# The output part of a linear-attention layer, traced in two pieces around the next step's matrix inverse

## The chip, the cores and the metric

The kernel runs on one core of one Trainium2 chip. Its time is the device time in microseconds of one execution; the time before is 3139.35 us, the median of three runs (3136.95 to 3140.87). Five engines work side by side, each through its own instruction stream in a fixed order: TensorE (PE; its weight loads are listed as PEld), VectorE (DVE), ScalarE (ACT), GpSimd (POOL) and SyncE (SP, which here only issues DMAs).

## The reference

Two layers over a sequence of 2048 tokens with 1024 channels. Only the first matters here. Its main branch is an RWKV-7 time mixing with 12 heads of width 64: each head keeps a 64 x 64 state, and per token

```
z = h @ a_w_in                      # projections, shifted in time by one token
state = state*w + sa (kk*a)^T + v k^T,   sa = state @ (-kk)
y = state @ r                       # per head
y = (y - mean(y)) * rsqrt(var(y) + LNX_EPS) * lnx_w + lnx_b
y = (y + bonus) * silu(gate)        # then one output projection with the memory branch
```

Beside it there is a cross-attention into 256 memory tokens; the second layer is a differential attention. Neither is touched.

## The kernel before

The first layer (`layer_a`) works on pairs of heads (6 pairs, index p) and on blocks of 512 tokens (4 blocks, in two halves of the sequence). One pair on one block is a `Step`; there are 24, in the order half, pair, block. A step treats its 512 tokens as 8 chunks of 64 and computes them in chunked form. Its parts are methods, and they are named here by what the prediction needs:

- `p1` (lines 334 to 395): the projections of the pair, each 24 matmuls of 128x512 (line 174), and elementwise work on them. `gate` is one more projection and a SiLU (lines 300 to 308). A step has four such projections, 96 matmuls, in all.
- `p2` (397 to 429): the chunk products `Gm` (PSUM tiles `pg`), transposes, and the bonus `bon`.
- `p3` (431 to 468): on DVE, the inverse of the 16 x 16 diagonal blocks. It ends in two DVE transposes, `T16` (line 462) and `TT16` (line 466).
- `p3b` (470 to 503): the rest of the inverse, a chain that goes back and forth between engines: PE products of `E1` and `T16` (line 481, first use) - ACT copy to `E1` (483) - PE products of `E1` and `TT16` (481, second use) - DVE add into `TT` (484) - DVE transpose `Ta` (487) - PE `invz` (494) - ACT copies (496) - PE `invr` (500) - DVE copies into `TT` (502).
- `p4` (508 to 564): PE transposes `atp` (520) and products `nvp` (528), ACT copies of both to `X` (522, 530), products with `TT` (`txp`, 539), and the chunk transition matrices (`mrp`, `ch`).
- `p4b` (566 to 590): the run over the 8 chunks, PE and ACT in turn (574, 575), then the output `ys` of the step (588, 590).
- `p5` (592 to 616): the normalisation of `ys` on DVE (597 to 608, with two small ACT operations at 605 and 606), then four PE transposes into `py` (611), an ACT scale and bias (613), the DVE addition of `bon` (614), the POOL product with the gate (615) and the store to DRAM, issued from POOL (616).

The main loop (lines 733 to 766) traces for step i: `p2` and `p3` of step i+1, `p4b` and `p5` of step i, `p3b` and `p4` of step i+1, and then `filler(i + 2)`, which holds the gate of step i+1 and `p1` of step i+2. The filler is where the long runs of projection matmuls come from.

Three things set the order. First, the place in the trace of the program is a rank: a list scheduler goes through a modelled run when the program is built and gives each engine the first-traced of the instructions that the model takes to be ready. So projection matmuls of the filler, traced last, stand between the products of `p3b` in PE's stream. On the chip that order is fixed, and an engine whose next instruction isn't ready waits. Second, the PSUM tiles of all these parts except the projections come from one ring of three buffers (tag "gm", `PS` at line 253). In the order of tracing, around the change, they are: `pvt`, `yp`, `yp`, `py`, two tiles `inv` (the two products of line 481), `invz`, `invr`, `atp`, `nvp`, `txp`, `txp`, `mrp`, `mrp`. The projections have their own three buffers (tag "pj"). Third, some tiles have one buffer only, `ys` among them, which the next step's line 590 writes again.

The steps 0, 10 and 11 differ from the others: the second half of the sequence starts with step 12, its input must first be normalised and transposed, and there are few projections left to put between.

Of the kernel before, what the change touches and what calls it, by code (L numbers as in the profile page):

```python
# [59 lines left out]
def hybrid_kernel(ctx, tc, S, HALF, x, mem, pv, cv, dist, postn, w_out, w_mkv, a_w, w2, a2, w_kv, b_w, out):  # L60
# [21 lines left out]
    def pc(name, i=0, n=1):  # L82
        return pvt[:, PV[name] + i:PV[name] + i + n]
# [41 lines left out]
    def split(ps, hi, lo):  # L125
        A.activation(hi, ps, AF.Copy)  # L126
        V.tensor_tensor(out=lo, in0=ps, in1=hi.bitcast(F32), op=ALU.subtract)
# [81 lines left out]
    def layer_a(ph):  # L209
# [31 lines left out]
        def T(shape, name, bufs=1, tag=None, dt=F32):  # L241
            return pa.tile(shape, dt, name=name, tag=tag or name, bufs=bufs)
# [10 lines left out]
        def PS(shape, name, tag="gm", bufs=3):  # L253
            if tag == "pj":
                return ppj.tile(shape, F32, name=name, tag="pj", bufs=3)
            return pps.tile(shape, F32, name=name, tag=tag, bufs=bufs)
# [69 lines left out]
        class Step:  # L326
# [263 lines left out]
                    A.activation(ys[:, :, hh], py[hh], AF.Copy)  # L590

            def p5(self):
                p, ys, sil = self.p, self.ys, self.sil
                bs = T([P, 8, 6], "bs", 1)
                y8 = ys.rearrange("p j h v -> p (j h) v")
                for i in range(8):
                    V.bn_stats(out=bs[:, i, :], in_=y8[:, i, :])
                sm = T([P, 4, 8], "sm", 1)
                V.tensor_tensor(out=sm[:, 0], in0=bs[:, :, 1], in1=bs[:, :, 4], op=ALU.add)
                V.tensor_tensor(out=sm[:, 1], in0=bs[:, :, 1], in1=bs[:, :, 4], op=ALU.subtract)  # L600
                V.tensor_tensor(out=sm[:, 2], in0=bs[:, :, 2], in1=bs[:, :, 5], op=ALU.add)
                V.scalar_tensor_tensor(out=sm[:, 3], in0=sm[:, 1], scalar=16.0, in1=sm[:, 1], op0=ALU.mult, op1=ALU.mult)
                V.tensor_tensor(out=sm[:, 2], in0=sm[:, 2], in1=sm[:, 3], op=ALU.add)
                V.tensor_scalar(out=sm[:, 0], in0=sm[:, 0], scalar1=0.5, scalar2=None, op0=ALU.mult)
                A.activation(sm[:, 3], sm[:, 2], AF.Ln, bias=eps_t[:, 1:2], scale=1.0 / 64)
                A.activation(sm[:, 3], sm[:, 3], AF.Exp, scale=-0.5)
                V.tensor_tensor(out=y8, in0=y8, in1=sm[:, 0, :, None].broadcast_to([P, 8, 64]), op=ALU.subtract)
                V.tensor_tensor(out=y8, in0=y8, in1=sm[:, 3, :, None].broadcast_to([P, 8, 64]), op=ALU.mult)
                py = PS([P, NJ, P], "py")
                for j in range(NJ):  # L610
                    nc.tensor.transpose(py[:, j, :], ys[:, j].rearrange("p h v -> p (h v)"), ident)
                yo = ys.rearrange("p j h v -> p (j h v)")
                A.activation(yo, py.rearrange("p j t -> p (j t)"), AF.Identity, bias=pc("lnx_b", p), scale=pc("lnx_w", p))
                V.tensor_tensor(out=yo, in0=yo, in1=self.bon, op=ALU.add)
                G_.tensor_tensor(out=yo, in0=yo, in1=sil, op=ALU.mult)
                G_.dma_start(out=y_dram[p * P:(p + 1) * P, self.t0:self.t0 + TB], in_=yo)

        def mem_w(m):
            return [load_a(c0) for c0 in (2432 + BR + m * P, 2432 + BR + MEMW + m * P)]

        def mem_q(m, half, bs, ws, between=lambda: None):
            for b in bs:
                def gate():
                    between()
                    return gate_silu(pj(ws[1], hTs[half, b]), W([P, TB], "g_sil"))
                store_q(0, m, half * NB + b, pj(ws[0], hTs[half, b]), gate, W)

        ths, steps = {}, []
# [28 lines left out]
        n = NHALF * NPAIR * NB  # L657
# [70 lines left out]
        def load_wo(hf):  # L728
            wo_w.append([ph.tile([P, KT, TB], F32R, name="wo" + t_, tag="h" + t_) for t_ in ("hi", "lo")])
            for c in range(0, 512, P):  # L730
                split_w(pa, w_out[0][:, hf * 512 + c:hf * 512 + c + P], None, *(t_[:, :, c:c + P] for t_ in wo_w[hf]), V, None, "iv", 4)

        for i in range(n):
            if i + 1 < n:
                steps[i + 1].p2()
                steps[i + 1].p3()
            steps[i].p4b()
            if i == n - 1:
                load_wo(0)

                yr0 = T([P, NC, P], "yr0", 2, "AR")[:, 0:NHB]
                nc.sync.dma_start(out=yr0, in_=y_dram[:, 0:P].rearrange("(k p) t -> p k t", p=P))
                y0 = T([P, KT, P], "yh0", 1, "BKT", F32R), T([P, KT, P], "yl0", 2, "AR", F32R)
                split(yr0, y0[0][:, 0:NHB], y0[1][:, 0:NHB])
                kv0 = T([P, 4, ML], "kb0", 2, "UV", F32R), T([P, 4, ML], "vm0", 2, "UV")[:, 0:2]
                G_.dma_start(out=kv0[0], in_=mem_d[0][0])
                nc.sync.dma_start(out=kv0[1], in_=mem_d[0][1])
                q0 = T([P, 2, 4, 2, P], "mq0", 2, "Gm", F32R)[:, 0]
                for dup in range(2):
                    G_.dma_start(out=q0[dup * 64:dup * 64 + 64], in_=q_d[0][0][0])  # L750
                g0 = T([P, 4, P], "mg0", 2, "bon")[:, 0:2]
                nc.sync.dma_start(out=g0, in_=q_d[0][1][0])
                for m in range(2):
                    mem_q(m, NHALF - 1, [NB - 1], ws[m])
                stl.close()
                op = OutProj(0, y_dram, x, x1_dram, 3, y0=y0, m0=(kv0, (q0, g0)))
            steps[i].p5()
            if i + 1 < n:
                steps[i + 1].p3b()
                steps[i + 1].p4()  # L760
            if i + 2 <= n:
                filler(i + 2)
            if i == n - 2:
                ws = [mem_w(m) for m in range(2)]
                for m in range(2):
                    mem_q(m, NHALF - 1, range(NB - 1), ws[m])
# [508 lines left out]

    ph = ExitStack()
    op = layer_a(ph.enter_context(pool_(name="ph", bufs=NB)))
    const2 = ctx.enter_context(pool_(name="const2", bufs=1, side="right"))
    ones = const2.tile([P, P], F32, name="ones")
# [103 lines left out]
```

## Time and profile before

| | before |
|---|---|
| median of 3 runs | 3139.35 us (3136.95 to 3140.87) |
| the profiled execution, its own time | 3131.17 us |
| its span | 3129.4 us |
| granted TensorE clock, mean | 0.979 |
| PE busy | 2944.0 us (94%) |
| DVE busy | 1794.5 us (57%) |
| ACT busy | 1504.3 us (48%) |
| POOL busy | 840.2 us (27%) |

The span runs from the first to the last recorded instruction; the 1.8 us around it belong to the execution's own time. The profiled execution was 8.2 us faster than the median of the three timed runs. A busy PE is one with a matmul under way by the profile, whose matmul ends are modelled; where successive matmuls overlap it counts as busy throughout, and the idle time in brackets ahead of an instruction is what is left. Steps 0 to 23 of the first layer end between 180 us and 1462 us of the span, about 50.2 us apart in the regular stretches.

### The profile page before, as it was taken

How to read it: one execution, taken by the hardware profiler on the slowest of the kernel's cores; microseconds unless marked ns; L12 is line 12 of the kernel's file. 1: busy time of each engine (PE TensorE's matmuls, PEld its weight loads, DVE VectorE, ACT ScalarE, POOL GpSimd, SP SyncE). 2: the span in 40 equal slices, each digit the busy share in tenths (PEclk: the TensorE clock that was granted, in tenths of full speed). 3: DMA queues.
4: the chain of work that ended last, by engine and by line, in shares of the span. 5: the costliest groups of instructions: out<-in, count | busy, mean ns of one | idle time of the engine just before them, and what ended most of it. 6: DMA issues, size and time to landing. Idle time of an engine off the chain costs nothing. (4 is left out here: it accounts for less than half of the span.)

```text
span 3129.4 us, 57336 instructions
## 1 busy us (share of the span) xinstructions
PE 2944.0 (94%) x22378; PEld 2390.8 (76%) x22378; DVE 1794.5 (57%) x4728; ACT 1504.3 (48%) x3310; POOL 840.2 (27%) x881
## 2 busy tenths in 40 slices
PE   6889999997899999998999999999999999998999
PEld 4767777776677777777777798888887888786777
DVE  6566767655676767673565311101118988887554
ACT  5545454545545454444454513213226777776443
POOL 3143423432243433431001212302212222323000
PEclk8899999998899999999999999999999999999999
DMA  3211000122011000115544533433355455543453
GB/s 119 78 33 37 28 24 23 39 61 84 26 30 37 28 24 24 38 45 142 147 135 127 147 86 91 118 86 92 102 164 123 101 113 115 122 85 103 129 153 116
DMA packets 262895, 264.13 MB, mean 84 GB/s; under 512 B 16736, under 2 KB 203232, under 8 KB 262496
## 3 DMA queue, kind: packets, MB, share of 16 engines
q1 hardware_dynamic: 234464, 193.87, 21.4%
q0 software_dynamic: 28160, 66.60, 10.4%
q8 instruction: 176, 2.88, 0.4%
q14 instruction: 95, 0.78, 0.1%
HBM read 179.14 MB, written 81.26 MB: 83 GB/s over the span
## 5 line engine op out<-in xcount | busy, mean ns | idle before, releaser
L174 PE MATMUL pj<-hhi,wh 128*128 128x512 f32 x928 | 389.6, 420 | 9.2 <-ACT sil L301 2.6
L174 PE MATMUL pj<-hhi,wl 128*128 128x512 f32 x928 | 375.3, 404 | 0.6 <-POOL wl L123 0.6
L174 PE MATMUL pj<-hlo,wh 128*128 128x512 f32 x928 | 368.5, 397 | 0.0
L123 POOL TENSOR_TENSOR wl<-wraw,wh 128x512 fp32r<-128x512 f32 x160 | 210.5, 1325 | 497.2 <-ACT wh L122 477.3
L1200 DVE CUSTOM_DVE_ANT_0 E<-s,dist 128x512 f32<-128x512 f32 (+1 forms) x480 | 276.1, 605 | 35.0 <-PE s L1198 28.9
L174 PE MATMUL pj<-bh,wh 128*128 128x512 f32 x672 | 262.8, 391 | 0.0
L174 PE MATMUL pj<-bh,wl 128*128 128x512 f32 x672 | 262.6, 391 | 0.0
L174 PE MATMUL pj<-bl,wh 128*128 128x512 f32 x672 | 262.5, 391 | 0.0
L1205 ACT ACTIVATE E<-E,nm 128x1920 f32<-128x1920 f32 (+7 forms) x192 | 229.4, 1199 | 59.1 <-DVE nm L1203 58.6
L174 PEld LDWEIGHTS pj<-hhi,wh 128*128 128x128 f32 x928 | 175.8, 189 | 63.7 <-ACT sil L301 8.9
L1238 PE MATMUL o<-th,vs 128*128 128x256 f32 (+1 forms) x864 | 211.0, 376 | 2.3 <-ACT th L1231 0.9
L1197 PE MATMUL s<-ks,qd 128*128 128x512 f32 (+1 forms) x480 | 205.6, 432 | 2.2 <-DVE mx L1200 1.2
L174 PEld LDWEIGHTS pj<-hhi,wl 128*128 128x128 f32 x928 | 175.4, 189 | 40.7 <-POOL wl L123 1.5
L174 PEld LDWEIGHTS pj<-hlo,wh 128*128 128x128 f32 x928 | 176.2, 190 | 38.8 <-issue 5.5
L122 ACT ACTIVATE wh<-wraw 128x512 fp32r<-128x512 f32 x160 | 100.3, 627 | 217.0 <-PE pj L174 139.4
L1238 PEld LDWEIGHTS o<-th,vs 128*128 128x128 f32 x864 | 153.9, 189 | 38.3 <-ACT th L1231 18.8
L1198 PE MATMUL s<-ks,qd 128*128 128x512 f32 (+1 forms) x480 | 176.1, 373 | 0.0
L174 PEld LDWEIGHTS pj<-bh,wh 128*128 128x128 f32 x672 | 126.7, 189 | 26.4 <-DVE ot L936 0.3
L174 PEld LDWEIGHTS pj<-bh,wl 128*128 128x128 f32 x672 | 126.6, 188 | 26.3
L174 PEld LDWEIGHTS pj<-bl,wh 128*128 128x128 f32 x672 | 126.6, 188 | 26.1
L1231 ACT ACTIVATE th<-tr 128x512 f32<-128x512 f32 (+1 forms) x216 | 113.2, 568 | 44.1 <-PE tr L1228 43.7
L1208 DVE SCALAR_TENSOR_TENSOR E<-E,nm,E 128x1920 f32<-128x1920 f32 (+7 forms) x96 | 132.1, 1376 | 0.9
(421 smaller groups left out, 6983.8 us busy)
## 6 DMA issues: line engine op xcount, KB each, us to landing
wraw<-in_a_w SPq DMA_DIRECT2D x118, 256.0 KB, 2.9
qd<-qd_d POOLq DMA_DIRECT2D x48, 512.0 KB, 7.0
mq<-mq POOLq DMA_DIRECT2D x64, 256.0 KB, 4.6
yr<-y_dram SPq DMA_DIRECT2D x32, 384.0 KB, 5.0
ks<-ks_d POOLq DMA_DIRECT2D x24, 512.0 KB, 7.0
xt<-in_x SPq DMA_DIRECT2D x16, 512.0 KB, 5.5
x_dram<-ot SPq DMA_DIRECT2D x16, 512.0 KB, 4.3
wraw<-in_b_w SPq DMA_DIRECT2D x32, 256.0 KB, 3.0
```

Of the source, the lines that this page charges most:

```text
L122: A.activation(hi[:, ks], raw, AF.Copy)
L123: eng.tensor_tensor(out=lo[:, ks], in0=raw, in1=hi[:, ks].bitcast(F32), op=ALU.subtract)
L174: mm(ps, lhsT=w[a_][:, k, wcol], rhs=h[b_][:, k, tsl], start=n == 0, stop=n == 3 * KT - 1)
L1197: mm(ps[:, f:f + w_], lhsT=qd[:, 0, c, qs], rhs=k_[:, c, 0:w_], start=True, stop=False)
L1198: mm(ps[:, f:f + w_], lhsT=qd[:, 1, c, qs], rhs=k_[:, c, 0:w_], start=False, stop=True)
L1200: V.tensor_tensor_reduce(out=e[:, kb * 512:kb * 512 + w], in0=ps[:, 0:w], in1=dt_[:, u0:u0 + w], scale=-SLOPES[h], scalar=3.0e38, op0=ALU. ...
L1205: A.activation(E[c][:, 0:nk], E[c][:, 0:nk], AF.Exp, bias=nm[:, c:c + 1], scale=-1.0, accum_out=nm[:, 2 + c:3 + c])
L1208: V.scalar_tensor_tensor(out=E[0][:, 0:nk], in0=E[1][:, 0:nk], scalar=nm[:, 5:6], in1=E[0][:, 0:nk], op0=ALU.mult, op1=ALU.add)
L1231: A.activation(th[:, 0:w], ps[:, 0:w], AF.Copy)
L1238: mm(po[:, oc], lhsT=vs[kt // 4][:, kt % 4, :], rhs=th[:, rc], start=n == 0, stop=n >= nmm - 2, skip_group_check=True)
```

## The change

`p5` ends after the normalisation. The rest, from the transposes to the store, becomes a method of its own, `p5b`, and the loop traces it after `p3b` of the next step and ahead of its `p4`. No instruction is added or taken away. In the ring of PSUM buffers `py` now comes after `invr` and before `atp`. For the last step nothing comes between the two parts.

```
             def p5(self):
-                p, ys, sil = self.p, self.ys, self.sil
+                ys = self.ys
...
                 V.tensor_tensor(out=y8, in0=y8, in1=sm[:, 3, :, None].broadcast_to([P, 8, 64]), op=ALU.mult)
+
+            def p5b(self):
+                p, ys, sil = self.p, self.ys, self.sil
                 py = PS([P, NJ, P], "py")
                 for j in range(NJ):
                     nc.tensor.transpose(py[:, j, :], ys[:, j].rearrange("p h v -> p (h v)"), ident)
...
             steps[i].p5()
             if i + 1 < n:
                 steps[i + 1].p3b()
+            steps[i].p5b()
+            if i + 1 < n:
                 steps[i + 1].p4()
             if i + 2 <= n:
                 filler(i + 2)
```

## Rows read from the trace of the kernel before

**Rows 1.** The page: engine busy time, share of the span, instructions.
```profile
PE 2944.0 (94%) x22378; PEld 2390.8 (76%) x22378; DVE 1794.5 (57%) x4728; ACT 1504.3 (48%) x3310; POOL 840.2 (27%) x881
```
**Rows 2.** Stages: start and end, length, each engine's busy time, granted clock, DMA.
```profile
282.00:735.00 453.00, 428.77 (x4528) 343.72 (x4528) 294.92 (x786) 220.41 (x490) 163.74 (x150) 1.00 0.14 41
735.00:882.00 147.00, 116.34 (x1135) 92.67 (x1135) 95.50 (x254) 71.42 (x166) 39.76 (x38) 0.87 0.13 40
```
**Rows 3.** Waits of PE, 180 to 1442 us: total us, times, longest.
```profile
PE py L611 <- DVE ys L608: 24.0, 23, 2.3
PE inv L481 <- DVE T L462: 13.9, 3, 6.1
...
PE invz L494 <- DVE Ta L487: 4.3, 10, 1.4
...
PE pj L174 <- ACT sil L301: 2.6, 10, 0.3
```
**Rows 4.** PE in step 4, in order: start, length, operation [idle before, releaser].
```profile
397.03 0.50 PE L174 MATMUL pj<-hhi,wh 128*128 128x512 f32 x1 [0.26 <-ACT sil L301]
...
398.98 0.40 PE L174 MATMUL pj<-hhi,wl 128*128 128x512 f32 x1
400.59 0.63 PE L611 MATMUL py<-cvt,ys 128*128 128x128 f32 x4 [1.22 <-DVE ys L608]
401.15 1.15 PE L481 MATMUL inv<-T,E 64*64 64x64 f32 x32
...
403.37 1.15 PE L481 MATMUL inv<-TT,E 64*64 64x64 f32 x32
...
409.06 1.09 PE L520 MATMUL atp<-cvt,AR 128*64 128x128 f32 x16
410.09 1.15 PE L528 MATMUL nvp<-UV,Gm 64*64 64x64 f32 x32
```
**Rows 5.** DVE in the same step.
```profile
395.62 0.17 DVE L603 TENSOR_TENSOR sm<-sm 128x8 f32<-128x8 f32 x1
...
395.82 1.08 DVE L462 STREAM_TRANSPOSE T<-X 128x512 f32<-128x512 f32 x1
...
398.60 1.07 DVE L466 STREAM_TRANSPOSE TT<-X 128x512 f32<-128x512 f32 x1
399.52 0.92 DVE L608 TENSOR_TENSOR ys<-ys,sm 128x512 f32<-128x512 f32 x1
...
409.90 0.84 DVE L502 COPY TT<-invr 32x256 f32<-32x256 f32 x2
```
**Rows 6.** ACT in the same step.
```profile
395.67 0.63 ACT L122 ACTIVATE wh<-wraw 128x512 fp32r<-128x512 f32 x1 [2.70 <-PE pj L174]
396.21 0.29 ACT L605 ACTIVATE sm<-sm,eps_t 128x8 f32<-128x8 f32 x1
396.40 0.57 ACT L301 ACTIVATE sil<-pj 128x512 f32<-128x512 f32 x1
...
402.54 0.58 ACT L483 ACTIVATE E<-inv 128x512 f32<-128x512 f32 x1
```
**Rows 7.** DVE in step 5.
```profile
445.91 1.08 DVE L462 STREAM_TRANSPOSE T<-X 128x512 f32<-128x512 f32 x1
...
447.44 1.08 DVE L466 STREAM_TRANSPOSE TT<-X 128x512 f32<-128x512 f32 x1
```
**Rows 8.** PE in step 5.
```profile
451.00 0.63 PE L611 MATMUL py<-cvt,ys 128*128 128x128 f32 x4 [0.86 <-DVE ys L608]
```
**Rows 9.** PE in step 11.
```profile
831.83 0.66 PE L611 MATMUL py<-cvt,ys 128*128 128x128 f32 x4 [1.51 <-DVE ys L608]
...
842.03 1.97 PE L481 MATMUL inv<-T,E 64*64 64x64 f32 x32 [3.77 <-DVE T L462]
```
**Rows 10.** Two stretches after such waits, columns as in rows 2.
```profile
196.50:199.90 3.40, 3.40 (x36) 2.51 (x35) 0.82 (x3) 3.12 (x6) 1.27 (x1) 0.50 0.00 0
841.60:848.50 6.90, 6.47 (x70) 5.32 (x71) 3.63 (x8) 4.53 (x8) 1.36 (x3) 0.51 0.01 2
```

More of the change, by code (lines that the diff above doesn't have):

```diff
@@ L592, in p5 @@
             def p5(self):
-                p, ys, sil = self.p, self.ys, self.sil
+                ys = self.ys
                 bs = T([P, 8, 6], "bs", 1)
@@ L608, in p5, with p5b @@
                 V.tensor_tensor(out=y8, in0=y8, in1=sm[:, 3, :, None].broadcast_to([P, 8, 64]), op=ALU.mult)
+            def p5b(self):
+                p, ys, sil = self.p, self.ys, self.sil
                 py = PS([P, NJ, P], "py")
@@ L759, in layer_a @@
                 steps[i + 1].p3b()
+            steps[i].p5b()
+            if i + 1 < n:
                 steps[i + 1].p4()
```

## The prediction

> **What bounds the kernel now.** The page comes first: PE is busy 94% of the span, the next engine 57% [rows 1]. So time is won where PE idles, or where it works slowly. The stages tell how much idle time there is: from 282 to 735 us, nine regular steps, PE is busy 428.8 of 453.0 us at a full clock, which leaves 24.2 us, 2.7 us a step; from 735 to 882 us, around the turn to the second half of the sequence, it idles 147.0 - 116.3 = 30.7 us and the mean granted clock is 0.87 [rows 2]. Then the waits of PE say what ends the idle time. The largest group is exactly what is edited: the transposes into `py` wait for the last normalisation on DVE (line 608), 24.0 us in 23 waits. The second is the first product of `p3b` waiting for `T16`, 13.9 us, but in three waits only [rows 3]: the steps 0, 11 and 10.
>
> The regular steps come in two kinds, by the block. In even ones, step 4 for all nine, PE issues the last of nine projection matmuls at 398.98 and then stands 1.22 us for line 608; the product of `T16` follows behind the transposes at 401.15, the second product at 403.37 [rows 4]. In odd ones, step 5 for eight, the wait is 0.86 us (0.79 to 0.88) [rows 8]. The steps 9 and 21 wait 0.3 us, step 22 2.27.
>
> One more thing is to be seen in step 4. `T16` is complete at 395.82 + 1.08 = 396.90 [rows 5], 4.25 us before its product starts, and nine projection matmuls of lower rank stand between. The scheduler would have put the product ahead of them if it could. What held it is the ring of three PSUM buffers: its `inv` tile comes behind `py` there, so it has no buffer before `py` has one. That is what the change takes away.
>
> **The change, part by part.** No work is added: the four transposes (0.63 us of PE), the ACT operation, the addition, the product and the store are the same. PE has as many turns from projections to small matmuls as before, since the transposes go from the front of the first product to the front of `atp`. So PE's work is the same and the sum goes over its waits.
>
> *Removed.* Line 608's wait ahead of the transposes: 1.22 us in nine steps, 0.86 in eight. Behind the inverse the normalisation is long done. With it should go the 0.26 us that the projection at 397.03 waits for ACT [rows 4], since the product of `T16` will stand about there; and the 0.33 us by which `invz` waits for `Ta` in the nine even steps (3.0 of the 4.3 us in [rows 3]; 1.36 is step 10), because the scan that DVE does between `TT` and `Ta` there isn't ready yet when `TT` comes some 4 us earlier.
>
> *Added: a wait for `T16`.* DVE doesn't get faster, and where PE's order follows the modelled run it will now stand at the product. How long depends on how far the model is from the chip at that point, and ACT's order shows it. In step 4 ACT took the weight copy (line 122) at 395.67 first, then line 605 and then the gate's copy (301) [rows 6]. Line 122 waits for the end of the gate's projection. Line 605 needs line 603, and has the higher rank, so in the model 603 ended after 122 was taken and before it was through, that is 0 to 0.5 us behind the projection's end. On the chip 603 ended at 395.79 [rows 5], 0.1 us behind. The chip is on the model's time there, or ahead of it. `T16` takes 1.08 us from there. If the model gives it 0.6 (my estimate, from what the whole way to line 608 must take in the model: the nine matmuls and those of `lr` run from 395.7 to 399.2, so at most some 3 us, where the chip needs 4.65), the model has `T16` 0.7 to 1.2 us behind the projection and the chip 1.2. Bounds for the wait at the first product: 0, and 1.2 if it is put right behind the gate's projection. I take 0.25 in even steps and 0.3 in odd ones, nearest to what line 603 shows.
>
> *Added: a wait for `TT16`.* The second product needs `TT16`, 398.60 + 1.07 = 399.67 in step 4 [rows 5]. The first product would run from 397.0 to 398.15, ACT copies in 0.58 us [rows 6], and the model, which has `TT16` earlier, puts some three matmuls between: PE stands at the second product from about 398.9. That is a wait of 0.8; bounds 0 and 1.5 (399.67 less the first product's end). I take 0.9 with the latency. In odd steps `TT16` comes 1.53 us after `T16` [rows 7] instead of 2.77, and the ACT copy ends no earlier: 0.1.
>
> *Behind it.* The second product comes at about 399.8 instead of 403.4, and the whole chain with it, 3.6 us earlier. This gives nothing by itself: PE has projections to do in place of it, before or after. The transposes now stand between `invr` and `atp`, and delay `atp` by 0.6; the projections cover that too. On ACT line 613 (0.76 us) comes ahead of the copies to `X`, while PE does `atp` (1.09 us), which covers it. On POOL the product with the gate and the store come about as late as the second product now does plus 3 us; behind them there stand only weight splits of the filler, for which PE waits nowhere in [rows 3]. The buffer `ys` is written again 45 us later.
>
> *The ring.* `nvp` gets the buffer of `invr`, which DVE frees (line 502), where before it had that of `invz`. In step 4 line 502 ends at 410.74 [rows 5]; `nvp` would be issued 0.57 us later than the 410.09 of before [rows 4], at 410.66. So 0.1 us a step; bounds 0, and 1.2 if DVE has the scan (1.23 us in this step) under way. I take 0.1.
>
> *Sum of the regular steps.* Even: 1.22 + 0.26 + 0.33 go, 0.25 + 0.9 + 0.1 come: 0.56 us, nine times, 5.0. Odd: 0.86 goes, 0.3 + 0.1 + 0.1 come: 0.36, eight times, 2.9. Step 22: 2.27 goes, perhaps half comes back: 1.1. Steps 9 and 21: nothing. Together 9.0 us.
>
> *The three steps of the turn.* In step 11 PE waits 1.51 us for line 608 and then, with 25 matmuls between, 3.77 for `T16` [rows 9]. Taking the first wait away lets PE reach the second earlier and stand there longer, so nothing is won; the transposes (0.66 us) pass from a time when PE has to wait anyway to behind the inverse. In step 10 nothing is left to fill and they lengthen the chain, by 0.66 to 1.1 us. Step 0 is like step 11. I take 1 us of loss for step 10. The clock: after the waits in step 0 and step 11 it is at half, the 1.2 GHz level, for 3.4 and 6.9 us, with PE busy 3.40 and 6.47 us of these [rows 10]. One such stretch more, of 3.4 us, costs 1.7 us of work; I take 1 us for the two steps together, from 0 to 3.4.
>
> The Trainium skill (TensorE: Matmul & The Clock Gate, section "What's actually happening") says that the throttled state is the default and that activity releases it. By that rule the longer hole at `T16` (3.77 + 1.51 + 0.6 = 5.9 us in step 11) must lengthen the slow stretch in both steps, the full 3.4 us; by the rows alone the stretch stays as it is. The sum would be 4.6 us gained by the one, 8.0 by the other.
>
> In all 9.0 - 1 - 1 = 7.0 us are gained: 3124.2 us for the profiled execution of 3131.17 us (3122.4 of span). The median of the runs lies 8.2 us higher, and I carry the difference over to it: 3132.4, say **3132 us**.
>
> **The rivals.**
> *A: the forecast*, gains of 2 to 14 us. Chance 0.45.
> *B: the wait only moves.* PE's order is laid down by a model that is 1.5 us ahead of DVE by line 608, and what is saved there is stood out at `T16` and `TT16` in full. For it: in step 11 just that must happen; against it: line 603 is on time, and between it and line 608 other work can be put. 3139, within 4 us. Chance 0.19.
> *C: the waits vanish.* 24.0 less the 3.4 of the three steps of the turn and 0.6 of the steps 9 and 21, with 2.6 and 3.0: 25.6 us less 2: about 3115. It needs the first product to fall on or after `T16` on the chip. For it: 603 is early, if anything; against it: `TT16` falls 2.77 us later in even steps. Chance 0.15.
> *D: the ring and the order cost more than the wait.* With `nvp` bound to line 502, and line 502 behind the scan or a mix on DVE, PE stands up to 1.2 us in each of 20 steps; the model, in which the copies are short, doesn't fill the time. At 1.0 us each and with B's zero gain: 20 us, less what the odd steps escape, about 14 with the slow clock: 3153. It decides from the point where that wait is over 0.5 us, the mean gain of a step (9.0 / 20). For it: 502 comes within 0.1 us of `nvp` already. Against: DVE is idle between the parts of the inverse. Chance 0.18.
> *E: nothing changes in PE's order*, because something other than the ring holds the first product behind the transposes: 3139. Chance 0.03.
>
> **How the numbers follow.** About 0.2%, 6.3 us, is what a measurement of this kernel tells from no change. Faster by more: C and two thirds of A, 0.45. Within: the rest of A, B and E, 0.37. Slower: D, 0.18. The range goes from 3115, C's value, to 3147, short of D's: it leaves out half of C and rather more than half of D, 0.2. A alone would be 3125 to 3137.
>
> **What will show it.** In the profile after: the wait of line 611 for line 608 gone from the list; the first product of line 481 ahead of the transposes, some 4 us earlier after the end of `yp`; waits for `T16` and `TT16` on line 481 of together about 1.1 us in even steps and 0.4 in odd ones; the transposes between lines 500 and 520; PE idle from 282 to 735 us down by 4 us. I am wrong if line 481 still stands behind line 611, if its new waits reach 1.5 us a step, if line 528 waits for line 502 by more than 0.5, or if the stretch of the turn grows by more than 4 us.

## The result, and the profile after

The changed kernel takes **3159.3 us** (median of four runs, 3157.3 to 3160.32) against 3138.94 us for the kernel before in the same job: a ratio of **1.0064**, 95% interval 1.0051 to 1.0076. It is slower by about 20 us, where 3132 was forecast, 7 us faster; the time lies above the range.

From the page of the kernel after, the counterpart of [rows 1]:

```profile
PE 2967.7 (94%) x22378; PEld 2403.1 (76%) x22378; DVE 1786.8 (57%) x4728; ACT 1505.7 (48%) x3310; POOL 830.7 (26%) x881
```

The same instructions, and PE is *busy* 23.7 us longer. The spans of the profiled executions are 29.1 us apart (3158.5 and 3129.4), more than the medians, since the one before lay 8.2 us below its median. The stages, with the columns of [rows 2], in stretches that do about the same work as those of before (steps 1 to 9, the turn, steps 13 to 22):

```profile
290.00:757.00 467.00, 435.26 (x4499) 346.09 (x4496) 294.51 (x783) 218.50 (x486) 159.79 (x148) 0.97 0.14 40
757.00:904.00 147.00, 120.18 (x1157) 95.99 (x1155) 96.20 (x257) 72.30 (x168) 42.78 (x41) 0.86 0.14 41
904.00:1415.00 511.00, 479.04 (x5363) 379.23 (x5361) 345.28 (x930) 241.03 (x524) 183.80 (x174) 0.98 0.10 29
```

Before, the regular steps ran at a granted clock of 1.00 (share of the full 2.4 GHz, rounded); the last of these three stages was, in the kernel before:

```profile
882.00:1385.00 503.00, 471.65 (x5361) 376.75 (x5360) 348.77 (x931) 239.34 (x525) 188.57 (x175) 1.00 0.10 30
```

The count of matmuls and the idle time are nearly the same (5361 and 5363; 31.4 and 32.0 us), but it takes 8 us more, with the clock at 0.98. The waits of PE after, 180 to 1442 us (the counterpart of [rows 3]; line 611 is now line 614):

```profile
PE inv L481 <- DVE T L462: 27.7, 23, 6.1
PE ch L574 <- ACT S L575: 24.4, 33, 2.7
PE pg L406 <- DVE Gm L408: 11.1, 12, 1.7
...
PE inv L481 <- DVE TT L466: 3.9, 6, 1.5
...
PE pss L367 <- ACT rn L359: 2.5, 8, 0.6
...
PE invz L494 <- DVE Ta L487: 1.7, 2, 1.4
...
PE txp L539 <- ACT X L530: 0.5, 1, 0.5
```

The 24.0 us of the transposes into `py` have gone. In their place stand the wait for `T16` (13.9 before) and one that was small: the state products of `p4b` (line 574) waiting for the state that ACT copies (line 575), 24.4 us now and 5.2 before. The wait at `txp`, 9.7 us before, is all but gone. The two rows of the kernel before:

```profile
PE ch L574 <- ACT S L575: 5.2, 14, 2.4
...
PE txp L539 <- ACT X L530: 9.7, 20, 0.5
```

Where it happens is seen in PE's instructions. First the end of `yp` in the kernel before (step 4, just ahead of [rows 4]), then, in the kernel after, a step whose inverse goes as forecast (step 5):

```profile
391.90 0.33 PE L588 MATMUL yp<-S,RT 64*64 64x64 f32 x4
```

```profile
452.32 0.33 PE L588 MATMUL yp<-S,RT 64*64 64x64 f32 x4
457.22 1.15 PE L481 MATMUL inv<-T,E 64*64 64x64 f32 x32 [0.26 <-DVE T L462]
...
464.70 0.66 PE L614 MATMUL py<-cvt,ys 128*128 128x128 f32 x4
```

The first product of the inverse starts 4.57 us behind the end of `yp`; in the kernel before it was 8.9 us (392.23 to 401.15 in [rows 4]). The whole chain, with `p4` at its end, is some 4 us earlier. The next rows show what then follows `p4`, first in the kernel before (step 4, behind [rows 4]), then in the kernel after (step 3):

```profile
408.08 0.39 PE L174 MATMUL pj<-hhi,wl 128*128 128x512 f32 x1
408.40 0.73 PE L500 MATMUL invr<-TT,Ta 32*32 32x32 f32 x32
...
415.27 1.15 PE L563 MATMUL ch<-UV,BKT 128*64 128x64 f32 x32
416.35 1.12 PE L367 MATMUL pss<-rn,cvt 128*128 128x512 f32 x2
```

```profile
367.57 1.15 PE L563 MATMUL ch<-UV,BKT 128*64 128x64 f32 x32
...
370.15 0.39 PE L174 MATMUL pj<-hhi,wl 128*128 128x512 f32 x1
370.38 0.33 PE L574 MATMUL ch<-sb,MT 128*128 128x64 f32 x2
372.33 0.43 PE L574 MATMUL ch<-S,MT 128*128 128x64 f32 x2 [1.63 <-ACT S L575]
373.17 0.43 PE L574 MATMUL ch<-S,MT 128*128 128x64 f32 x2 [0.41 <-ACT S L575]
374.21 2.07 PE L367 MATMUL pss<-rn,cvt 128*128 128x512 f32 x2 [0.60 <-ACT rn L359]
...
376.51 0.63 PE L174 MATMUL pj<-hlo,wh 128*128 128x512 f32 x1
376.94 0.63 PE L174 MATMUL pj<-hhi,wl 128*128 128x512 f32 x1
```

The projection that ends at 408.5 in the one and at 370.5 in the other is `kx`, the first of the next `p1` in the trace. `pss` (line 367) is a matmul on an elementwise result of `kx`, and in the order of PE the projections `rx` and `vx` come behind it. In the kernel before, `pss` follows 7.9 us behind the end of `kx` (8.3 in the other kind of step): in that gap PE does the end of the inverse and all of `p4`, and waits less than 1 us in all. In the kernel after this differs from step to step. In every second one, as here, `p4` is over *before* `kx` ends. The gap from `kx` to `pss` is 3.7 us in the first half of the sequence and 2.9 in the second, and what the scheduler found for it are three state products of the next `p4b`. Two of them wait for ACT, here 1.63 and 0.41 us, and `pss` waits 0.60 behind them. In the steps between, `kx` still ends ahead of the last part of `p4`, and `pss` follows that without a wait, 4.9 us behind `kx` (step 4):

```profile
421.12 0.40 PE L174 MATMUL pj<-hhi,wl 128*128 128x512 f32 x1
...
425.36 1.15 PE L563 MATMUL ch<-UV,BKT 128*64 128x64 f32 x32
426.44 1.13 PE L367 MATMUL pss<-rn,cvt 128*128 128x512 f32 x2
```

There it is DVE that is late, with `T16`, ahead of the inverse of the same step:

```profile
408.61 1.97 PE L481 MATMUL inv<-T,E 64*64 64x64 f32 x32 [2.19 <-DVE T L462]
...
411.10 0.63 PE L174 MATMUL pj<-hhi,wh 128*128 128x512 f32 x1
```

Beside both waits the granted clock falls to half, 1.2 GHz instead of 2.4: the product of 1.15 us takes 1.97, `pss` takes 2.07 for 1.12, and projection matmuls start 0.43 us apart (376.51, 376.94) where 0.23 is usual. The windows say the same (columns as in [rows 2]):

```profile
374.40:377.80 3.40, 3.40 (x7) 2.04 (x8) 0.69 (x1) 0.72 (x2) 0.58 (x1) 0.53 0.32 95
408.60:412.00 3.40, 3.39 (x36) 3.05 (x37) 2.13 (x6) 1.95 (x4) 0.78 (x3) 0.54 0.31 89
```

Summed from the traces for each stretch from one end of `yp` to another (before, after; us):

| ends of `yp`, steps | matmuls | length | PE idle | PE busy | at half clock |
|---|---|---|---|---|---|
| 1 to 9 | 4288 | 405.0, 422.2 | 25.5, 32.0 | 379.5, 390.3 | 6.8, 34.1 |
| 9 to 12 (turn) | 1912 | 247.4, 249.8 | 32.4, 31.4 | 215.0, 218.4 | 37.5, 44.4 |
| 12 to 22 | 5360 | 503.2, 511.0 | 31.3, 32.0 | 471.8, 479.0 | 3.4, 17.1 |

The two regular rows are 25.1 us longer: 7.1 us more of idle time, and 18.0 us more of busy time for the same matmuls. The time at half clock is 41.0 us longer; half of that, 20.5, is about what the busy time gained. By the wait that stands next to each fall of the clock, 30.7 of the 51.2 us at half clock go with the state products, 10.2 with `T16`, and 10.2 with `pg`.

Of the 29.1 us there remain 4.4 us ahead of the end of `yp` in step 0, 2.6 won in step 1, 2.4 lost in the turn, and 0.1 won behind step 22. The 4.4 us are not the change's: up to 186 us of the span the instructions of PE, ACT, DVE and POOL stand in the same order in both kernels.

### The profile page after: what moved, and what is told of

It reads as the page before. It is cut to its first block, busy times and chain, and to the rows that moved or that the text cites. A ratio compares the mean times of both kernels' runs of the same rounds, so it can differ in the third digit from the quotient of the medians.

```text
span 3158.5 us, 57321 instructions
## 1 busy us (share of the span) xinstructions
PE 2967.7 (94%) x22378; PEld 2403.1 (76%) x22378; DVE 1786.8 (57%) x4728; ACT 1505.7 (48%) x3310; POOL 830.7 (26%) x881
## 4 chain that ended last, share of the span: by engine, by line
PE 71%; DVE 13%; ACT 7%; issue 4%; DMA 3%; POOL 1%; SPq 0%; ACTq 0%; DVEq 0%; POOLq 0%
PE pj L174 29%; PE po L930 10%; PE o L1243 5%; PE vps L1106 4%; PE s L1202 3%; PE s L1203 2%; PE tr L1233 2%; PE inv L481 2%; PE mo L866 1%; DMA wraw<-in_a_w 1%; DVE Ti L455 1%; DVE E L1205 1%; DVE itmp L453 1%; PE mpt L859 1%; PE pss L367 1%
## 5 line engine op out<-in xcount | busy, mean ns | idle before, releaser
L174 PE MATMUL pj<-hhi,wh 128*128 128x512 f32 x928 | 396.6, 427 | 8.5 <-DVE hlo L149 1.8
L1243 PEld LDWEIGHTS o<-th,vs 128*128 128x128 f32 x864 | 154.0, 189 | 37.9 <-ACT th L1236 18.6
```

Source lines behind the costliest of these rows:

```text
L174: mm(ps, lhsT=w[a_][:, k, wcol], rhs=h[b_][:, k, tsl], start=n == 0, stop=n == 3 * KT - 1)
L1243: mm(po[:, oc], lhsT=vs[kt // 4][:, kt % 4, :], rhs=th[:, rc], start=n == 0, stop=n >= nmm - 2, skip_group_check=True)
```

## The experiments

Theory T, formed from this: the change does shorten the chain, and the chain was what covered the elementwise work that follows `kx`. With less cover, PE meets a hole, and what fills or fails to fill it sets the time. At first T reached from `kx` to `pss` only; the way on from `pss` to the chunk products `pg` was added after a_rx_first and a_pss_gm had missed. The rivals: R1, the drawn-forward state products are themselves the cost; R2, the transposes and the buffer of `py` in the middle of the chain are.

### The state products held back (a_chunks_late)

The state products (line 574) may be issued on PE only behind the last transposes of `p2`, so none can be drawn ahead of `pss` (dots stand for code in between):

```
-                    nc.tensor.transpose(pv_[:, j, :], self.vx[:, j * P:(j + 1) * P], ident)
+                    Step.last = nc.tensor.transpose(pv_[:, j, :], self.vx[:, j * P:(j + 1) * P], ident)
...
-                    mm(ch[:, c, :], lhsT=MT[:, c, :], rhs=st[c], start=False, stop=True, skip_group_check=True)
+                    with tc.issue_after(Step.last.ins):
+                        mm(ch[:, c, :], lhsT=MT[:, c, :], rhs=st[c], start=False, stop=True, skip_group_check=True)
```

> The changed kernel, with the state products of the next step (line 574) held behind the last transposes of p2 on PE, in issue order only, so that none of them can be drawn forward. In the changed kernel every second step has three of them drawn forward into the time between the first projection and the product pss (line 367). Theory T (the inverse and p4 now end 3.6 us earlier, and so no longer cover the time that pss waits for the elementwise work on the first projection; the next projections have to wait for pss, which stands ahead of them in their PSUM ring): the idle time stays and turns up as a wait of line 367 in all regular steps, some 2.5 to 3.5 us in each of 20; 3155 to 3185 us. Rival R1 (the early state products themselves are the cost, by their waits and by what they do to the order of the next step): 3120 to 3137 us. Rival R2 (the new place of py in the ring of three buffers, and of the transposes between invr and atp, is the cost): 3153 to 3165 us, with no large wait of line 367.

3185.86 us (3183.93 to 3210.86), ratio 1.0181 (1.0136 to 1.0226), 0.9 us above T's range and far above those of R1 and R2: with nothing drawn forward the time rises, and a large wait stands at line 367. R1 is out, and R2 doesn't explain this wait. The waits of PE:

```profile
PE pss L367 <- ACT rn L359: 61.7, 20, 3.2
```

With the state products gone, `pss` waits 2.9 to 3.2 us in *each* of 20 steps, and stands 2.9 to 3.2 us behind `kx`, just as long as the elementwise work takes. Here the hole is in every step; in the changed kernel the state products stood in it in every second one and `p4` in the others.

This run also tells about the wait for `T16`: between the ends of `yp` 1 to 9 and 12 to 22 it comes to 17.2 us in the changed kernel, and here to 4.9 in as many waits (18, about 0.27 each). So the late `T16` comes with the drawn-forward order and isn't what makes the hole. How much of the 20 us it carries no run shows.

### The hole filled with matmuls that are thrown away (a_busy)

Twelve projection-sized matmuls write into the tile of `pss` just before it; their result is overwritten.

```
                 pss = PS([P, TB], "pss", "pj")
+                for k in range(0 if first else 12):
+                    mm(pss, lhsT=ws[0][0][:, k % KT, :], rhs=h[0][:, k % KT, :], start=True, stop=True)
```

> The changed kernel with 12 extra projection matmuls (2.7 us, of operands that are there, into the PSUM tile of pss, which pss then overwrites: work that is not used) ahead of pss in each step but those of the first pair. With them nothing is drawn forward, and PE's order is that of a_chunks_late but for the 12 matmuls, which stand where that kernel waits 3.1 us at pss. So PE waits as long, but working. Theory K (half of the loss is TensorE's clock, which falls to half after waits of 2 us and more, as it was for 51 us of the regular steps in a_chunks_late and 14 us in the kernel before): 3186 less 15 to 20, 3160 to 3173 us, granted clock of the regular steps near that of before. Rival (the wait alone counts, the slow clock falls into it): 3182 to 3192 us.

3164.04 us, ratio 1.0099 (1.0079 to 1.0119), as theory K expected. The state products stay behind `pss` here too, so a_chunks_late is the one to compare with: 22 us *less* with twelve matmuls *more* in each of 20 steps (240; the four steps of the first pair have none). First a_chunks_late, then a_busy, 300 to 740 and 900 to 1400 us:

```profile
300.00:740.00 440.00, 402.07 (x4280) 318.46 (x4280) 274.67 (x705) 202.07 (x437) 151.69 (x139) 0.98 0.12 35
900.00:1400.00 500.00, 455.83 (x4960) 359.56 (x4959) 330.28 (x884) 222.54 (x484) 169.75 (x162) 0.96 0.09 26
```

```profile
300.00:740.00 440.00, 426.18 (x4437) 339.65 (x4436) 275.46 (x713) 208.48 (x452) 152.99 (x143) 1.00 0.13 37
900.00:1400.00 500.00, 482.43 (x5355) 383.41 (x5351) 334.55 (x912) 234.99 (x511) 167.80 (x162) 1.00 0.09 27
```

The clock is whole again and the idle time more than halved (37.9 + 44.2 us to 13.8 + 17.6). A pair of steps took 105.8 us and takes 103.5: in the first half, 6.1 us of idle time and 1.7 of clock (half of 3.4) less, 5.4 of matmuls more (24 at 0.227, as they follow each other in this trace). The matmuls take up about the time that was idle; what is won is mostly the clock. By the Trainium skill (TensorE: Matmul & The Clock Gate, section "What's actually happening") throttling is the default and activity lifts it; the two kernels agree (a granted clock of 0.98 and 0.96, then 1.00).

The expectation's "after waits of 2 us and more" does not hold as a bound. In the kernel before, the clock fell to half beside single waits of 1.12 to 1.14 us at `pg` three times in the regular steps (at 278, 381 and 1282 us); in a_chunks_late it stayed full beside eight of the 3.23 us waits at `pss`.

### `rx` ahead of `pss` (a_rx_first, b_rx_first)

Useful work in the hole: the second projection traced ahead of `pss`, in the changed kernel and in the one before.

```
-                first = p == 0
+                first = True
```

> The changed kernel, with the second projection (rx) of every step traced ahead of pss, as the kernel has it already for the first pair: 24 projection matmuls (5.4 us) that need no pss. Theory T: the uncovered time is filled, no state product is drawn forward, PE loses its waits at lines 611, 574 and 367: 36 us less than with the waits, 3100 to 3127 us. R1: also 3105 to 3130, since nothing is drawn forward. R2: no lower than 3143 us, since the transposes and their ring are where they were.

3174.45 us, ratio 1.0122 (1.0107 to 1.0137).

> The control: the kernel before, with the same second projection ahead of pss. Theory T: there pss was covered by p4 already, so only the 0.5 us goes that PE waits at txp in each of 20 steps: 3122 to 3138 us. R1 and R2 the same. If it gains as much as the changed kernel does with it, the projection's place is worth that by itself and says nothing of the change.

3199.38 us, ratio 1.02 (1.018 to 1.0219). Both missed, 47 and 61 us above their ranges; the first lies where R2 had it. The rows of waits, of a_rx_first and of b_rx_first:

```profile
PE pg L406 <- DVE BK L383: 57.1, 21, 3.4
```

```profile
PE pg L406 <- DVE BK L383: 56.0, 21, 2.9
PE py L611 <- DVE ys L608: 20.1, 21, 1.5
```

`pss` doesn't wait any more, but the elementwise work goes on behind it (`rn`, `BK`, up to line 383), and only `vx` is left to do meanwhile. The hole has moved from `pss` to `pg`. The split's own part is visible beside it: 25 us between the two kernels.

### `pss` off the ring of the projections (a_pss_gm)

The tile of `pss` takes a buffer of the small tiles, so that `rx` can be ahead of it by one buffer more.

```
-                pss = PS([P, TB], "pss", "pj")
+                pss = PS([P, TB], "pss")
```

> The changed kernel, with pss in the ring of the small tiles (gm) instead of the projections' ring; the order of tracing is left as it is. Theory T: what held the projections back was that pss comes ahead of them in their ring, so freeing the ring is enough: 3100 to 3130 us, PE without waits at lines 574 and 367. R1: the same if nothing is drawn forward. R2: 3145 us or more. If projections are held by something else than the ring, 3153 to 3165 us.

3150.92 us, ratio 1.0043 (1.0028 to 1.0058): missed, though 8 us below the median of the change alone (the intervals of the two ratios just overlap). This time too lies where R2 had it; the waits tell the two apart, and so does the run with the transposes moved, below. Again the hole moves to `pg`:

```profile
PE pg L406 <- DVE AR L390: 40.3, 18, 3.2
```

Here `pg` starts 13.4 and 15.0 us in turn behind the end of `kx`, in a_rx_first 14.4 and 14.6, and waits each time. Behind `kx` a step has two projections more, 48 matmuls about 0.23 us apart: 11 us. The rest has to come from `p4`, as in the kernel before, or from elsewhere.

### The gate's projection in the place of the cover (a_gate2, a_gate3, each with and without the split)

The gate's projection of the step before depends on nothing in the step and was traced first in the filler, ahead of `kx`. It is traced third here (behind `rx`, with `t == 2` in the last line) or last (behind `vx`, `t == 3`), and `pss` takes the small tiles' ring as above.

```
-            if idx and not (first and b) and not (r == 0 and idx < n):
+            plain = idx and not (first and b) and not (r == 0 and idx < n)
+            mid = plain and idx < n
+            if plain and not mid:
                 steps[idx - 1].gate()
...
-                steps[-1].p1()
+                steps[-1].p1(lambda t: steps[idx - 1].gate() if mid and t == 3 else 0)
```

> The changed kernel with pss in the ring of the small tiles and the gate's projection of the step before traced behind the second projection (rx) instead of ahead of the first, in all steps but those of the first pair. By that the first projection runs some 5 us earlier against the inverse, so its elementwise work is again beside the inverse and p4, and 48 projection matmuls stand behind pss, as before. Theory T (the loss is the time from the first projection to pg that p4 no longer covers): no wait of 2 us is left in the regular steps, and the 24 us of line 611's wait are won: 3100 to 3124 us. Rival R2 (the transposes between invr and atp, and py's place in the ring, cost): 3145 us or more.

Third, with the split: 3134.59 us, ratio 0.9997 (0.9982 to 1.0011). T's range (3100 to 3124) was missed: `pg` still waits (16.1 us for `Gm`, 10.5 for `carry`), and `invz` 13.6 for `Ta`.

> The control of a_gate2_pss_gm: the kernel before with the same two moves. Line 611's waits of 0.9 to 1.2 us stay, the 0.5 us at txp may go, but only 38 matmuls stand between pss and pg, so some wait at pg can come: 3122 to 3160 us. If it is as fast as a_gate2_pss_gm, the two moves are worth that by themselves and the split of the output part nothing.

Third, without the split: 3183.39 us, ratio 1.0163 (1.0143 to 1.0182), above the expected range.

> As a_gate2_pss_gm, with the gate's projection behind the third projection (vx), last in its step. Theory T: as good, 3100 to 3126 us, for 47 or 48 matmuls stand behind pss here too; if the gate's SiLU is needed too early, a wait at line 615 on POOL, off PE's path. R2: 3145 us or more.

Last, with the split: **3112.26 us**, ratio **0.9932** (0.9913 to 0.9951), as T expected, and below both kernels.

> The kernel before (output stage in one part) with the two other moves of the faster variant: `pss` in the ring of the small tiles, and the gate's projection as the last of the four. In PE's order 38 to 40 projection matmuls (40 at 0.23 us: 9.1 us) stand between `pss` and the chunk products `pg`, where the variant with the split has 47 or 48. Theory T (the elementwise work between the end of the first projection and `pg` takes some 13.7 us, and what PE has to put into that time decides): `pg` waits some 2 to 3 us for DVE in nearly every step, as in the kernel before with the gate's projection third (57 us in all), `py` waits its 24 us as before: 3165 to 3190 us. Theory M (the two moves alone bring the gain, the split nothing): 3105 to 3130.

Last, without the split: 3146.98 us, ratio 1.0036 (1.0022 to 1.0049). Neither theory's number: my count of 40 matmuls left out that here `rx` too is done ahead of `pss`, so that `pss` comes 19.6 to 23.2 us behind `kx` and `pg` waits little (14.0 us for `Gm`, in nine waits). The stages with the gate last, first with the split and then without (the stretches differ a little in length):

```profile
288.00:738.00 450.00, 431.36 (x4523) 344.29 (x4521) 305.56 (x782) 221.96 (x490) 161.36 (x155) 0.99 0.15 44
...
896.00:1389.00 493.00, 470.02 (x5322) 373.43 (x5320) 356.56 (x921) 238.84 (x519) 179.88 (x175) 1.00 0.11 32
```

```profile
300.00:740.00 440.00, 418.90 (x4378) 333.49 (x4372) 289.11 (x730) 214.52 (x471) 156.69 (x148) 0.98 0.15 43
900.00:1400.00 500.00, 472.44 (x5302) 374.50 (x5300) 351.59 (x890) 236.99 (x510) 177.99 (x173) 0.97 0.10 30
```

And the first waits of each:

```profile
PE inv L481 <- DVE T L462: 26.4, 23, 5.7
...
PE pg L406 <- DVE Gm L408: 5.9, 9, 0.7
```

```profile
PE py L611 <- DVE ys L608: 24.9, 23, 2.5
PE pg L406 <- DVE Gm L408: 14.0, 9, 1.6
```

Where the hole has other cover, the split does what it is for. Between these two it is worth 34.7 us by the medians, 33 by the ratios (they ran in different jobs): over the stretches 0 to 9 and 12 to 22, the idle time falls from 54.9 to 43.5 us and the time at half clock from 58.0 to 13.7. With the gate third it is worth 48.8 us. In the kernel as it was, the same edit costs 20 us.

### The place of the transposes (a_out_behind_p4, a_gate3_out_behind)

Rival R2 by itself: the second part of the output stage behind `p4`, once in the changed kernel and once in the fastest one.

```
-            steps[i].p5b()
             if i + 1 < n:
                 steps[i + 1].p4()
+            steps[i].p5b()
```

> The changed kernel with the second part of the output stage traced behind `p4` and not ahead of it. In PE's order the four transposes into `py` come behind the products `ch`; the three state products drawn ahead of `pss` in every second step, and 48 projection matmuls behind `pss`, stay as they are. Theory T: the loss comes from the early inverse and the order that follows it, not from the transposes ahead of `atp` or from the buffer that `py` takes there: 3150 to 3168. Theory R2 (the transposes in the chain ahead of `atp`, 0.6 us each step, and the ring buffer they take, are the loss): 3130 to 3145.

3162.76 us, ratio 1.0084 (1.0069 to 1.0099): as T expects, and far from R2's 3130 to 3145. R2 is out. The three waits of line 574 are there as before (24.8 us, 34 times).

> The faster variant (split, `pss` in the ring of the small tiles, gate's projection last) with the second part of the output stage behind `p4`. PE's order is the same but for the four transposes. Theory T: the place of the transposes is worth less than 3 us, since the projections cover the 0.6 us: 3107 to 3117. Theory R2: the chain from `invr` to `ch` is 0.6 us shorter and PE waits for nothing else: 3095 to 3105.

3116.38 us (3105.66 to 3117.11), ratio 0.9931 (0.9912 to 0.995): no difference from the variant it is drawn from, and within T's range. Whether the transposes stand in the chain or behind it hardly matters.

### The gate last, without moving `pss` (a_gate3)

The diff of the fastest variant less the line of `pss`.

> The changed kernel with the gate's projection last, but `pss` left in the ring of the projections. In PE's order nothing stands between the two products of `p3b`, and 69 to 72 projection matmuls (16 us) stand in one run between `ch` and `pg`. Theory T: `pg` waits for nothing (16 us against 13.7), but the inverse is now uncovered: the second product waits for `TT16` (some 2 us less 0.6 in odd steps, 3 us in even ones) and `invz` for `Ta` and the copy (1.5 us or more), 4 to 6 us a step with the slower clock behind them: 3190 to 3260. Theory P (only the run behind `pss` counts, 48 matmuls or more are enough wherever the rest stands): 3105 to 3125.

3245.34 us, ratio 1.0346 (1.033 to 1.0362), as T expected. A long run of projections now stands between `ch` and `pg`, and none are left for the inverse:

```profile
PE inv L481 <- DVE T L462: 42.7, 21, 5.8
PE invz L494 <- DVE Ta L487: 31.4, 21, 1.9
```

The cover is a fixed stock: 96 projection matmuls a step, and two elementwise chains, the inverse and the way from `kx` to `pg`, that both need part of it. Here it all went to one of them. The idle time over the stretches 0 to 9 and 12 to 22 rises to 108.1 us and the time at half clock to 208.

## Why the prediction was wrong

*What bounds the kernel* was read rightly: PE, with its idle time and its clock.

*Removed waits*: right. The wait of `py` (24.0 us) is gone, the 0.33 us at `invz` too, and 9.2 us at `txp` that I hadn't counted. The first product stands ahead of the transposes, 4.3 us earlier behind `yp`, as forecast. That agrees with the buffer ring having held it; no run tested the ring by itself.

*Added waits*: right in size where a step is undisturbed (0.26 us for `T16` where 0.25 and 0.3 were taken; about 0.48 for `TT16` in the steps that have it, where 0.9 and 0.1 were), wrong in every second step. There PE waits 2.15 to 2.19 us for `T16` in the first half and 1.14 to 1.43 in the second. The sum had 4.7 us for `T16` in the regular steps, 17.2 were measured. What delays it in the first half is in the last section; in the second half it stays open.

*The step that failed* is the one headed "Behind it": that the earlier chain "gives nothing by itself: PE has projections to do in place of it", put into the sum as nothing won and nothing lost. The projections that would have covered it, `rx` and `vx`, stand behind `pss` in PE's order, and `pss` hangs on `kx`. I looked at what the moved chain waits for and at what stands inside it. I did not look at what *it* had been covering: the 7.9 us between the end of `kx` and `pss` in the rows of before were filled by the end of the inverse and `p4`, and to take 4 us out of a gap that ACT and DVE need is to open a hole. One row, 408.08 against 416.35, would have told it: `pss` had no wait in the list because its releaser had long been done. (The other half of that paragraph held: that the transposes between `invr` and `atp` are covered is what a_out_behind_p4 and a_gate3_out_behind show.)

*The clock* was priced for the steps 0 and 11 alone (1 us). The longer busy time is 18.0 us of the 25.1 in the regular steps, where the clock was at half for 10.2 us before and no wait was over 1.23 us, and for 51.2 us after, when waits of 1.3 to 2.2 us had come in. A sum over idle time, however well done, would have found little more than a quarter of the loss: PE's idle time in the stages 282 to 735 before and 290 to 757 after went from 24.2 to 31.7 us, where I had it falling by 4.

*The turn*: 2 us of loss were taken, with step 0, and 2.4 were lost between the ends of `yp` 9 and 12. That is luck. The hole at `T16` did not grow, it shrank: from 3.77 to 1.16 us in step 11 and from 3.98 to 2.67 in step 0. So the rule that the prediction cites was not put to the test there. The time at half clock went from 37.5 to 44.4 us all the same; 6.8 us of it now stand beside the wait of 2.6 us at `pg` ahead of step 12, where the kernel before had such a wait at full clock.

*The rivals*: D named about the right time (3153), by another mechanism: line 528 has no wait at all in the list after, so the buffer of `invr` isn't it. Its cause, an order in which PE stands where the model has something ready, was the right family. B, C and E are out: the wait didn't move to `T16` and `TT16` in full, it didn't vanish, and the order did change.

*Left open*: why the scheduler's order alternates between two kinds of step, and why the same waits at the state products are followed by the low clock in some steps (at 374 us) and not in others (about 478 us).

## What to carry to other kernels

Before a chain is pulled forward, look at what it was covering: take the operations of the same engine that follow it, and read how long ago their operands came to be needed, not only whether they wait. A matmul without a wait may be one that stands behind eight microseconds of other work. If the engine's clock depends on being kept busy, count the slow stretch that may follow a new wait of one or two microseconds (some 1.7 us of work lost in each 3.4 us here), and test an order by filling the hole with throwaway work: if that makes the kernel faster, the hole costs more than its idle time.

## What the runs showed of the hardware

Twelve matmuls more in each of 20 steps made a kernel 22 us faster (3185.86 to 3164.04). They took the place of idle time, and the time at half clock over the stretches 0 to 9 and 12 to 22 fell from 51.2 to 13.7 us, which is worth about 19.

A DVE operation beside a POOL one can take almost four times as long. Line 460, two operations that take 0.73 us in nearly all steps, took 2.65 to 2.69 in four steps of the kernel after, the four in which weight splits of the filler on POOL fell on it, for 2.40 to 2.45 us. DVE, then POOL:

```profile
404.71 2.69 DVE L460 TENSOR_SCALAR X<-Ti,cvt 128x256 f32<-128x256 f32 x2
407.43 1.04 DVE L462 STREAM_TRANSPOSE T<-X 128x512 f32<-128x512 f32 x1
```

```profile
404.53 1.29 POOL L123 TENSOR_TENSOR wl<-wraw,wh 128x512 fp32r<-128x512 f32 x1 [8.76 <-ACT wh L122]
...
405.83 1.33 POOL L123 TENSOR_TENSOR wl<-wraw,wh 128x512 fp32r<-128x512 f32 x1
```

The 1.96 us more are PE's wait for `T16` in these steps (2.19 us) less the 0.26 of an undisturbed one. The Trainium skill (SBUF — State Buffer, section "Who interferes with whom") says that VectorE in some of its modes and GpSimd use one pair of ports in turn, and the first to start holds it for its whole instruction. The trace agrees: POOL started 0.18 us ahead, and line 460 ended 0.24 us behind POOL's second operation. Which mode line 460 ran in is not in the trace.
